# Three edits in one kernel: memory preparation inside the first gemm, the first gather beside the router, expert scatters by matmul at seven pairs

## The chip, the cores and the metric

One NeuronCore of a Trainium2 chip. The metric is the device time of one execution in microseconds (us): the median of three runs. The profile is one further execution, with its own time.

The engines are PE (matrix multiply, into PSUM), DVE (elementwise, reductions), ACT (activations, copies), POOL (elementwise, and DMAs with indices), SP (here only a queue that issues DMAs). The kernel uses eight PSUM banks: four named pmm, three paux, one pacc.

## The reference

Two blocks over x (512 tokens of 1024). What touches the change:

```
first block:  h = rms_norm(x); u, v, sq, sk, sv, mq, z = split(h @ w_in)      # widths 512,512,256,128,128,256,1024
  y_a = gelu(u) * (w_spatial(causal) @ layernorm(gelu(v)) + b)                # in chunks of 128 tokens
  y_b = sliding window attention(sq, sk, sv) + relative bias, 4 heads
  mk, mv = split(rms_norm(mem) @ w_mem_kv);  y_c = attention(mq, mk, mv)      # mem: 256 rows of 1024
  x = x + rms_norm((concat(y_a, y_b, y_c) * silu(z)) @ w_out)
second block: sparse attention and a state space branch, merged (not touched), then the experts:
  g = argmax of 4 group logits; 2 best of the group's 8 experts; weights by softmax
  out[token] = sum over its 2 experts of  (silu(h @ gate_e) * (h @ up_e) * weight) @ down_e     # 32 experts, 1024 -> 256 -> 1024
  x = x + out
```

All arithmetic is float32. The 32 experts' weights are 192 units of 128x1024 (512 KB): per expert four of gate and up, two of down.

## The kernel before, in words

Most gemms split each operand into a high and a low part of a faster float type and run three products (L224 to L226, L269 to L271, L315 to L317). The weights are loaded raw (tile tb), copied to whi (L173, ACT) and subtracted to wlo (L175, DVE or POOL). The expert products take the raw float32 weights.

**Order.** The program is traced once in the order in which it is written, and a planner then gives each engine its queue: among the instructions that its own model of time calls ready it takes the one written first. Tiles of one tag (t2, tb, xe, y) share a fixed number of buffers. `mix(main, filler)` interleaves two generators: for each microsecond that a step of main asks for, steps of filler are written behind it. Within `manual_schedule(engines)` the written order holds on those engines.

**First block (L524 to L829).** x is loaded in eight pieces and split; eight squares are summed on POOL (L393). The first gemm (`gemm_r2`, L561) makes v for the gate; its norm comes in at its last step (L558). The memory rows are loaded on POOL's queue (L571). Then the products for k and v, q of the window, q of the memory (f1, L632) are written as filler of the layer norm (`ln_chain`) and the memory preparation (`mem_prep`, L574: square, split, sum, norm). `q_done` (L606) multiplies a product by the norm, which frees its PSUM banks, and stacks it. Behind that stand the bias, the memory's two gemms (L644, L645), and the attention of eight units, mixed with the gemms of u (two) and z (two); z[2] and z[3] follow.

**Router (`block2c`, L1402; `route`, L1525).** The last gemm runs in halves of 256 tokens; each half's tokens are transposed to rows (`rows`), its logits go to the plog bank and through `route`: on DVE the group maximum, the two best, one-hot rows; a small product on PE (L1563 to L1568) counts positions, giving posm. `moe_start` (L1853) asks for the first ten weight units, `moe` for eight more.

**Experts (`moe`, L1874).** Experts go in 16 pairs; each expert has 64 slots, 32 for each half of the tokens. `prep` writes the one-hot matrix of eight experts (L1657) and the slot weights; `gather_h` (first eight experts, by halves) and `gather` (the next groups, one group ahead) bring token rows to slots by matmul (L1709, L1725). Per pair: `gate_up` (L1738, 16 products), `act_t`, then one pair later `down` (L1759, 8 products). A weight tile that is used up is asked for anew by SP (`pair`, `moe_fetch`), 18 tiles in rotation.

The results of pairs 0 to 11 are stored in slot order to scratch memory (`y_store`), and after pair 11 each token fetches its two rows by index (`y_fetch`, L1780, eight fetches of 512 KB); a token whose expert is in another pair reads row 0 and multiplies it by zero. The results of pairs 12 to 15 are split (`y_split`) and added by matmul with the transposed one-hot rows (`slots_t`, `scatter`, `finish`): 12 and 13 together, then 14 and 15, and the rows go out.

```
        f1 = chain(self.gemm_t(u1(2), hh, hl, KK, kv_done), self.gemm_t(u1(3), hh, hl, KK, q_done(sq)),
                   self.gemm_t(u1(4), hh, hl, KK, q_done(mq)))
        mix(chain(self.ln_chain(av, vc), mem_prep()), f1)
```

Of the kernel before, what the change touches and what calls it, by code (L numbers as in the profile page):

```python
# [19 lines left out]
P = 128  # L20
T = 512
# [22 lines left out]
class Ker:  # L44
# [479 lines left out]
    def block1(self):  # L524
# [36 lines left out]
        run(self.gemm_r2([u1(0), u1(1)], hh, hl, [av_done(0), av_done(1)], norm))  # L561
        rb, rbh = r["b"], r["bh"]
        self.rvt1 = self.rows("rv1", self.px, nc.sync)

# [27 lines left out]
        m = {}  # L592
        skh, skl, sq, mq, mkh, mkl = [], [], [], [], [], []
# [40 lines left out]
        mix(chain(self.ln_chain(av, vc), mem_prep()), f1)  # L634
# [8 lines left out]
        nc.any.tensor_copy(sv, self.tpose([m["svT"][:, t * P:(t + 1) * P] for t in range(NT)]))  # L643
        run(self.gemm_t([("wm", 0), ("wm", 1)], mh, ml, KK, mk_done, n=256))  # L644
# [7 lines left out]
        st = {}  # L652
# [87 lines left out]


        ya = []
        bsp = self.rv("b_s").rearrange("p (g t) -> p g t", g=4)

        def u_done(g):
            def f(ps):
                us = [self.t2() for _ in range(2)]
                for u, p in zip(us, ps):
                    nc.vector.tensor_tensor(u, p, rb, op=ALU.mult)
                ss = []  # L750
                for c in range(2):
                    gi = 2 * g + c
                    pm = self.paux()
                    for t in range(NT):
                        nc.tensor.matmul(pm[:, t * P:(t + 1) * P], vc[t][:, gi * P:(gi + 1) * P],
                                         wtri[:, gi * P:(gi + 1) * P], start=True, stop=True)
                    s = self.t2()
                    nc.vector.tensor_tensor(g4(s), g4(pm), bsp[:, gi:gi + 1].to_broadcast([P, 4, P]), op=ALU.add)
                    ss.append(s)
                self.gelu2(us)  # L760
                for u, s in zip(us, ss):
                    nc.vector.scalar_tensor_tensor(s, s, 0.5, u, op0=ALU.mult, op1=ALU.mult)
                    ya.append(s)
            return f
# [3 lines left out]
        def z_done(g):  # L768
            def f(ps):
                zs = self.silu_from(ps, rbh)  # L770
                for c, z in enumerate(zs):
# [630 lines left out]
    def block2c(self, mh, ml):  # L1402
# [67 lines left out]
        for _ in self.route(0, self.rms_sum(self.ssq3, 0)):  # L1470
            pass
        rows(3, 0, 2)
# [4 lines left out]
        with self.norm1(True):  # L1477
# [21 lines left out]
            run(r)  # L1499
            self.route_end()  # L1500
# [24 lines left out]
    def route(self, h, pc):  # L1525
# [44 lines left out]
        nc.vector.tensor_tensor(self.posm[:, ts], pp[:, :64].rearrange("p (t e) -> p t e", t=2), mb, op=ALU.mult)  # L1570
        nc.vector.tensor_reduce(self.r["mx"][:, h:h + 1], pp[:, 64:96], axis=AX.X, op=ALU.max)
# [48 lines left out]
    def route_slots(self):  # L1620
# [13 lines left out]
        nc.vector.tensor_scalar(ok, sl, 1.0, None, op0=ALU.is_ge)  # L1634
        nc.vector.scalar_tensor_tensor(ok, sl, 64.0, ok, op0=ALU.is_le, op1=ALU.mult)
        nc.vector.scalar_tensor_tensor(ok, r["ei"], 24.0, ok, op0=ALU.is_lt, op1=ALU.mult)
        nc.vector.scalar_tensor_tensor(rw, r["ei"], 64.0, sl, op0=ALU.mult, op1=ALU.add)
        nc.vector.scalar_tensor_tensor(rw, rw, -1.0, ok, op0=ALU.add, op1=ALU.mult)
# [12 lines left out]
    def prep(self, b):  # L1651

        nc = self.nc
        oh = self.pg.tile([P, NT, 256], F32R, tag="oh", name=self.nm("oh"), bufs=1)
        for t in range(NT):
            i = self.iota1[:, t // 2 * 32:t // 2 * 32 + 32]
            nc.vector.tensor_tensor(oh[:, t].rearrange("p (e s) -> p e s", s=32),  # L1657
                                    i.unsqueeze(1).to_broadcast([P, 8, 32]),
                                    self.posm[:, t, 8 * b:8 * b + 8].unsqueeze(2).to_broadcast([P, 8, 32]),
                                    op=ALU.is_equal)  # L1660
        yield oh
        pc = self.paux()
        for q in range(2):
            for t in range(NT):
                o = 12 * (t // 2 * 2 + q)
                nc.tensor.matmul(pc[:, o:o + 12], oh[:, t, q * P:(q + 1) * P], self.wc[:, t, :, 12 * b + 6 * q:12 * b + 6 * q + 6],
# [17 lines left out]
    def slots_t(self, p):  # L1684
# [7 lines left out]
        o = self.pg.tile([P, T], F32R, tag="ohT", name=self.nm("ohT"), bufs=self.no)  # L1692
# [3 lines left out]
    def xtile(self, xe):  # L1696
        xe.append(self.pg.tile([P, 8, 64], F32, tag="xe", name=self.nm("xe"), bufs=self.nxe))

    def gather_h(self, oh, xe):

        nc = self.nc
        for h in range(2):
            for d in range(8):
                if h == 0:
                    self.xtile(xe)
                pg = (self.pmm if d % 2 else self.paux)()[:, :256]
                for t in (2 * h, 2 * h + 1):
                    for j, src in enumerate((self.hth, self.htl)):
# [491 lines left out]
```

## Time and profile before

| | |
|---|---|
| median of 3 runs | 1332.47 us (1329.52 to 1336.8) |
| profiled execution | 1331.22 us, span 1329.6 us, mean granted PE clock 0.981 |
| busy, share of the span | PE 1258.4 (95%), DVE 861.8 (65%), ACT 506.9 (38%), POOL 440.0 (33%) |
| DMA moved | 224.86 MB, mean 169 GB/s; in the expert slices mostly 415 to 416 |
| issues | 82 + 55 + 55 weight units of 512 KB, 12 stores and 8 fetches of results |

The span runs from the first to the last instruction of the core; the execution's time has 1.6 us around it. A line number is a line of the kernel before, and often a helper's. In a row, `out<-in` are tile names. `[2.77 <-DVE eq]` is the idle time of the engine just before the instruction, and what ended it. [...] Matmuls overlap, and a float32 product leaves two records, so the spacing of records counts and not their length.

### The profile page before, as it was taken

What the parts mean: (1) busy time and instruction counts of PE and PEld (TensorE: products, weight loads), DVE (VectorE), ACT (ScalarE), POOL (GpSimd) and SP (SyncE); (2) the same over time, 40 slices, a digit from 0 to 9 for tenths busy, and PEclk for the clock granted to TensorE, in tenths of its full rate; (3) what the DMA queues carried; (4) which work ended last, traced back from release to release, by engine and by line L of the source; (5) the groups of instructions that cost most, each with busy time, mean ns of one, the idle gap of its engine ahead of it and who ended that gap; (6) DMA issues with size and microseconds to landing.
All of it is one profiled execution on the core that took longest, in us unless ns stands there. A gap on an engine that the chain in (4) does not pass through costs nothing. (4 is left out here: it accounts for less than half of the span.)

```text
span 1329.6 us, 18774 instructions
## 1 busy us (share of the span) xinstructions
PE 1258.4 (95%) x6992; PEld 970.4 (73%) x6992; DVE 861.8 (65%) x1648; ACT 506.9 (38%) x938; POOL 440.0 (33%) x467
## 2 busy tenths in 40 slices
PE   5969999999999999999999999999999999998997
PEld 5857888989987888888777787877889744333323
DVE  5596765667999767777988788778583522111116
ACT  4535553355644455444444443443233211111011
POOL 5473133159344413113354343445324200000011
PEclk8979999999999999999999999999999899999999
DMA  7315233143233232034424334386330699999994
GB/s 253 111 54 154 64 97 110 48 145 95 79 96 119 80 97 78 25 115 125 119 88 115 107 96 135 98 280 177 122 142 24 245 416 416 397 416 415 416 414 179
DMA packets 87342, 224.86 MB, mean 169 GB/s; under 512 B 7840, under 2 KB 31040, under 8 KB 87248
## 3 DMA queue, kind: packets, MB, share of 16 engines
q1 hardware_dynamic: 79808, 203.08, 44.2%
q10 hardware_dynamic: 4992, 11.83, 2.3%
q0 software_dynamic: 2448, 8.72, 1.8%
q8 instruction: 56, 0.92, 0.3%
q14 instruction: 38, 0.31, 0.1%
HBM read 205.97 MB, written 17.63 MB: 168 GB/s over the span
## 5 line engine op out<-in xcount | busy, mean ns | idle before, releaser
L175 POOL TENSOR_TENSOR wlo<-tb,whi 128x1024 fp32r<-128x1024 f32 x78 | 199.6, 2560 | 319.5 <-ACT whi L173 293.1
L224 PE MATMUL pmm<-tb,whi 128*128 128x512 f32 x600 | 239.1, 399 | 1.8 <-DVE t L903 1.8
L225 PE MATMUL pmm<-tb,whi 128*128 128x512 f32 x600 | 237.2, 395 | 0.0
L226 PE MATMUL pmm<-tb,wlo 128*128 128x512 f32 x600 | 236.8, 395 | 0.0
L173 ACT CAST whi<-tb 128x1024 fp32r<-128x1024 f32 x139 | 145.0, 1046 | 143.4 <-PE pmm L225 57.1
L224 PEld LDWEIGHTS pmm<-tb,whi 128*128 128x128 f32 x600 | 114.0, 190 | 25.5 <-DVE t L903 2.2
L226 PEld LDWEIGHTS pmm<-tb,wlo 128*128 128x128 f32 x600 | 113.8, 190 | 23.8 <-issue 0.2
L225 PEld LDWEIGHTS pmm<-tb,whi 128*128 128x128 f32 x600 | 113.8, 190 | 23.1 <-issue 0.7
L175 DVE TENSOR_TENSOR wlo<-tb,whi 128x1024 fp32r<-128x1024 f32 x61 | 82.2, 1349 | 27.8 <-ACT whi L173 27.4
L224 PE MATMUL pmm<-t,whi 128*128 128x512 f32 (+1 forms) x208 | 80.2, 393 | 12.4 <-DVE t L610 12.4
L225 PE MATMUL pmm<-t,whi 128*128 128x512 f32 (+1 forms) x208 | 80.3, 389 | 0.8 <-DVE t L356 0.8
L226 PE MATMUL pmm<-t,wlo 128*128 128x512 f32 (+1 forms) x208 | 80.0, 388 | 0.0
L1745 DVE SCALAR_TENSOR_TENSOR th<-th,pmm 128x256 f32<-128x256 f32 x16 | 6.7, 420 | 102.6 <-ACT th L1744 102.6
L1262 DVE TENSOR_SCALAR t<-t,acs 128x128 f32<-128x128 f32 x128 | 41.8, 393 | 26.9 <-DMA t<-scr_a 26.7
L1183 DVE SCALAR_TENSOR_TENSOR t<-cv,cwh,t 128x512 f32<-128x512 f32 x72 | 58.5, 868 | 0.3 <-ACT t L1180 0.3
L1677 POOL COPY wcol<-wrow 32x2 f32<-32x2 f32 x64 | 12.0, 188 | 135.7 <-DVE y L1771 57.0
L1738 PE MATMUL pmm<-wr,xe 128*64 128x512 f32 x200 | 55.6, 597 | 0.6 <-DMA wr<-in_we_dram 0.6
L224 PEld LDWEIGHTS pmm<-t,whi 128*128 128x128 f32 x208 | 40.1, 193 | 20.0 <-issue 12.8
L334 PE MATMUL pmm<-whi,tb 128*128 128x256 f32 x192 | 54.7, 285 | 0.0
L336 PE MATMUL pmm<-whi,tb 128*128 128x256 f32 x192 | 54.5, 284 | 0.0
L335 PE MATMUL pmm<-wlo,tb 128*128 128x256 f32 x192 | 54.3, 283 | 0.0
L1744 ACT ACTIVATE th<-pmm,wcol 128x256 f32<-128x256 f32 x16 | 7.6, 474 | 113.1 <-PE pmm L1738 56.1
(446 smaller groups left out, 2969.2 us busy)
## 6 DMA issues: line engine op xcount, KB each, us to landing
wr<-in_we_dram SPq DMA_DIRECT2D x82, 512.0 KB, 10.0
tb<-in_w_dram SPq DMA_DIRECT2D x78, 512.0 KB, 3.7
rx<-in_we_dram SPq DMA_DIRECT2D x55, 512.0 KB, 9.0
tb<-in_we_dram SPq DMA_DIRECT2D x55, 512.0 KB, 10.1
tb<-in_wo_dram SPq DMA_DIRECT2D x16, 512.0 KB, 3.7
tb<-in_wg_dram SPq DMA_DIRECT2D x16, 512.0 KB, 3.6
t<-scr_a SPq DMA_DIRECT2D x16, 512.0 KB, 6.4
tb<-in_wsb_dram SPq DMA_DIRECT2D x16, 512.0 KB, 4.1
```

The lines of the kernel that those rows point to most:

```text
L173: nc.vector.tensor_copy(hi, raw) if dve_hi else nc.scalar.copy(hi, raw)
L175: f = lambda: (nc.gpsimd if pool_lo else nc.vector).tensor_tensor(lo, raw, hi, op=ALU.subtract)
L224: nc.tensor.matmul(ps[c][:, :n], hi[:, s], xh[k], start=first, stop=False)
L225: nc.tensor.matmul(ps[c][:, :n], hi[:, s], xl[k], start=False, stop=False)
L226: nc.tensor.matmul(ps[c][:, :n], lo[:, s], xh[k], start=False, stop=last)
L334: nc.tensor.matmul(o, xh[k][:, ts], hi[:, s], start=(k == 0 and t % 2 == 0), stop=False, **kw)
L335: nc.tensor.matmul(o, xh[k][:, ts], lo[:, s], start=False, stop=False, **kw)
L336: nc.tensor.matmul(o, xl[k][:, ts], hi[:, s], start=False, stop=(k == 7), **kw)
L1183: nc.vector.scalar_tensor_tensor(y, x[:, i:T + i], w(ct, i), y, op0=ALU.mult, op1=ALU.add)
L1262: nc.vector.tensor_scalar(h8(ab)[:, h], h8(ab)[:, h], self.acs[:, c, 8 * g + h:8 * g + h + 1], 0.0, op0=ALU.subtract, op1=ALU.min)
L1677: nc.gpsimd.tensor_copy(w[o:o + 32, i // 2, 0:2], wrow[e * 32:e * 32 + 32, 2 * h + q, e:5:4 - e])
L1738: nc.tensor.matmul(pg[h * 64:h * 64 + 64], xe[d][:, e + h], w[:, j * 512:(j + 1) * 512], start=(d == 0), stop=(d == 7))
```

## The change

**First block.** The loads of mem are written ahead of the first gemm, and the preparation is mixed into that gemm from its third step on; f1 is filler of the layer norm alone. The first u gemm, with its part of the gate, is written ahead of the memory's gemms. The attention's filler is the second u gemm and z[0], z[1], z[2].

**Router.** The one-hot of the first half (`oh_half(0, 0)`) is written ahead of the rows of the last 256 columns. Of `route(1)` only the part to the norm stays in `block2c`; then `moe` writes the first half's gather, the rest of the route, the second half's one-hot and gather, with all engines in written order.

**Experts.** PE is in written order to the end of the stage. Nine more weight units are loaded ahead, once, into three y, four xe and two ohT buffers, beside the 18 in rotation. Seven pairs (3, 6, 9, 12 to 15) are scattered by matmul, each for itself and two pairs after its products; nine are stored. Fetches have a bounds check: a token without a stored row has an index above the bound and its row is not moved; their four tiles are zeroed first. The one-hot is two tiles (one per half), xe eight double tiles, ohT two double tiles. `finish` begins the first four groups of pair 14 ahead of the last down products, and folds the residual by matmul in two groups instead of one.

```diff
@@ block1
-        run(self.gemm_r2([u1(0), u1(1)], hh, hl, [av_done(0), av_done(1)], norm))
...
+        f0 = self.gemm_r2([u1(0), u1(1)], hh, hl, [av_done(0), av_done(1)], norm)
+        for _ in range(2):
+            next(f0)
+        mix(mem_prep(), f0)
+        run(f0)
...
-        mix(chain(self.ln_chain(av, vc), mem_prep()), f1)
+        mix(self.ln_chain(av, vc), f1)
...
+        run(self.gemm_t(u1(5), hh, hl, KK, u_done(0)))
         run(self.gemm_t([("wm", 0), ("wm", 1)], mh, ml, KK, mk_done, n=256))
...
-        f2 = chain(*[self.gemm_t(u1(5 + g), hh, hl, KK, u_done(g)) for g in range(2)], z[0], z[1])
+        f2 = chain(self.gemm_t(u1(6), hh, hl, KK, u_done(1)), z[0], z[1], z[2])
         mix(self.pipeline(units, (logits, expo, ptrans, pvmul, otrans), 4.5), f2)
         run(f2)
-        run(z[2])
@@ block2c
         for _ in self.route(0, self.rms_sum(self.ssq3, 0)):
             pass
+        self.oh0 = self.oh_half(0, 0)
...
-            run(r)
-            self.route_end()
+            self.rt = r
@@ route_slots
+        nc.gpsimd.memset(base, 16384.0)
...
+        nc.vector.tensor_scalar(t2, ok, -16384.0, 16384.0, op0=ALU.mult, op1=ALU.add)
+        nc.vector.tensor_tensor(rw, rw, t2, op=ALU.add)
@@ oh_half, new
+        o = (self.pg if h else self.pa).tile([P, 2, 256], F32R, tag=f"slot{h}", name=self.nm("oh"), bufs=1)
+        for t in range(2):
+            nc.vector.tensor_tensor(o[:, t].rearrange("p (e s) -> p e s", s=32), i,
                                    self.posm[:, 2 * h + t, 8 * b:8 * b + 8].unsqueeze(2).to_broadcast([P, 8, 32]),
                                    op=ALU.is_equal)
@@ y_fetch
-            y = self.ytile()
+            y = self.yf[t % 2 * 2 + j]
-                ap=self.row1[:, t, j:j + 1], axis=0))
+                ap=self.row1[:, t, j:j + 1], axis=0), bounds_check=18 * 64 - 1, oob_is_err=False)
@@ finish
+        for t in range(NT):
+            early(0, t)
+        yield 1
+        for t in (0, 1):
+            early(1, t)
+        for t in range(NT):
+            late(0, t)
+        for t in (0, 1):
+            late(1, t)
+        for t in (2, 3):
+            early(1, t)
+            late(1, t)
@@ moe_start, moe_fetch
+        self.extra = [("y", self.ny)] * 3 + [("xe", self.nxe)] * 4 + [("ohT", self.no)] * 2
...
+            if n <= u < n + m:
+                tag, bufs = self.extra[u - n]
+                t = self.pg.tile([P, 1024], F32, tag=tag, name=self.nm("wr"), bufs=bufs)
+                self.nc.sync.dma_start(t, self.a["we"][e, i])
@@ moe, moe_body
+        self.direct = [3, 6, 9, 12, 13, 14, 15]
+        for _ in range(2 * self.nw + len(self.extra)):
+            self.moe_fetch()
+        with self.tc.manual_schedule(engines={pe}):
+            with self.tc.manual_schedule(engines=set(other)):
+                xe = []
+                self.gather_h(self.oh0, xe, 0)
+                next(self.rt)
+                next(self.rt)
+                oh = self.oh0, self.oh_half(0, 1)
+                run(self.rt)
+                self.route_end()
+                self.gather_h(oh[1], xe, 1)
+            self.moe_body(oh, xe)
...
+            if p == 16:
+                fin = self.finish()
+                next(fin)
+            if p:
+                if p == 1:
+                    ac = next(at.pop(0))
+                py = [self.pmm() for _ in range(2)]
+                for k in range(2):
+                    self.down(py, pair(p - 1, 4 + k), ac, k)
+                (self.y_split if p - 1 in self.direct else self.y_store)(p - 1, py)
+                if p < 16:
+                    ac = next(at.pop(p))
...
+                    if i == 2:
+                        xn = []
+                        gg = self.gather(oh, 8, xn)
+                    some(gg, 4)
+            if p > 1 and p - 2 in self.direct:
+                run(self.scatter((p - 2,)))
+            if p < 15 and p + 1 in self.direct:
+                self.slots_t(p + 1)
+            if p == 12:
+                self.yf = [self.pg.tile([P, 1024], F32, tag="xe", name=self.nm("yf"), bufs=self.nxe) for _ in range(4)]
+                for y in self.yf:
+                    nc.gpsimd.memset(y, 0.0)
@@ setup
-    k.fold = [(0, 0)]
+    k.fold = [(0, 3), (1, 1)]
-    k.nrx, k.ny, k.nxe, k.no = 5, 5, 16, 4
+    k.nrx, k.ny, k.nxe, k.no = 5, 5, 8, 2
```

## Rows read from the trace of the kernel before

**Rows 1.** The page's 40 slices: busy tenths of the 16 DMA engines.
```profile
DMA  7315233143233232034424334386330699999994
```

**Rows 2.** PE's waits, 0 to 200 us: us in total, times, longest.
```profile
PE pmm L224 <- DVE t L610: 12.4, 1, 12.4
...
PE pmm L316 <- DVE wlo L175: 6.1, 2, 5.7
```

**Rows 3.** Timeline of DVE, 60 to 135 us: start, us, line, [idle before <-releaser].
```profile
79.05 0.88 DVE L359 SCALAR_TENSOR_TENSOR t<-t,pvt,t 128x256 fp32r<-128x256 f32 x2
...
90.48 1.28 DVE L610 TENSOR_TENSOR t<-pmm,tb 128x512 f32<-128x512 f32 x2
```

**Rows 4.** Front: busy (x) of PE, PEld, DVE, ACT, POOL; PEclk, DMA, GB/s.
```profile
91.00:96.00 5.00, 4.70 (x24) 4.73 (x25) 4.23 (x8) 3.51 (x5) 1.06 (x1) 0.56 0.24 89
...
16.00:20.00 4.00, 1.61 (x10) 1.00 (x8) 4.00 (x4) 3.66 (x5) 3.84 (x4) 1.00 1.03 409
...
20.00:24.00 4.00, 0.00 (x0) 0.00 (x0) 4.00 (x2) 1.04 (x1) 4.00 (x3) 0.54 0.36 146
...
32.00:36.00 4.00, 4.00 (x35) 4.00 (x35) 0.00 (x0) 0.56 (x1) 0.00 (x0) 1.00 0.00 0
```

**Rows 5.** The same view and columns, from the router on.
```profile
1044.00:1048.00 4.00, 4.00 (x21) 4.00 (x21) 3.17 (x26) 0.95 (x3) 0.00 (x0) 0.53 0.56 226
...
1056.00:1064.00 8.00, 8.00 (x40) 2.69 (x38) 1.25 (x4) 0.47 (x1) 2.09 (x12) 1.00 0.83 273
...
1051.00:1288.00 237.00, 225.47 (x999) 92.63 (x999) 46.04 (x108) 31.65 (x62) 17.49 (x71) 0.99 1.00 399
```

**Rows 6.** Timeline of PE at the router.
```profile
1043.15 0.77 PE L1709 MATMUL paux<-oh,tb 128*128 128x256 f32 x2 [2.77 <-DVE eq L1546]
```

**Rows 7.** Chain of waits in order of time: start, us, what.
```profile
1054.26 13.88 PE pmm L1738 x64
...
1072.25 3.58 PE pmm L1759 x16
...
1082.70 0.37 PE paux L1750 x2
...
1084.01 1.88 PE paux L1725 x16
...
1176.01 11.36 DMA tb<-in_we_dram
...
1269.49 15.25 DMA wr<-in_we_dram
...
1286.36 0.47 PE paux L1837 x2
...
1313.87 1.86 PE pmm L1759 x4
...
1322.67 1.21 PE pacc L1808 x4
```

**Rows 8.** Timeline of SP's queue: start, us, line, x issues.
```profile
1033.72 4.81 SPq L1850 DMA_DIRECT2D wr<-in_we_dram  x4
...
1056.15 3.76 SPq L1850 DMA_DIRECT2D tb<-in_we_dram  x5
...
1292.44 1.61 SPq L1850 DMA_DIRECT2D wr<-in_we_dram  x2
```

**Rows 9.** The page's DMA issues: KB each, median us to landing.
```profile
wr<-in_we_dram SPq DMA_DIRECT2D x82, 512.0 KB, 10.0
...
scr_y<-y ACTq DMA_DIRECT2D x12, 512.0 KB, 7.0
```

**Rows 10.** Timeline of POOL, 0 to 60 us.
```profile
19.35 2.79 POOL L175 TENSOR_TENSOR wlo<-tb,whi 128x1024 fp32r<-128x1024 f32 x1
...
43.68 2.39 POOL L571 DMA_DIRECT2D t<-in_memT_dram  x4
```

**Rows 11.** Timeline of PE in the expert stage.
```profile
1246.16 3.40 PE L1759 MATMUL pmm<-rx,ac 128*64 128x512 f32 x4
```

More of the change, by code (lines that the diff above doesn't have):

```diff
@@ L651, in block1 @@
         sinks = self.rv("sinks")
-        st = {}
+        st, done = {}, set()
         def logits(u):
@@ L739, in otrans @@
                                   po[:, :256].rearrange("p (c t) -> p c t", c=2))
[L742 to L764, printed above, removed]
+            done.add(u)
         yh, yl = [], []
@@ L1691, in slots_t @@
         nc.tensor.matmul(pt, sel, self.posT, start=True, stop=True)
-        o = self.pg.tile([P, T], F32R, tag="ohT", name=self.nm("ohT"), bufs=self.no)
+        if self.direct.index(p) % 2 == 0:
+            self.oht = self.pg.tile([P, 2 * T], F32R, tag="ohT", name=self.nm("ohT"), bufs=self.no)
+        c = self.direct.index(p) % 2 * T
+        o = self.oht[:, c:c + T]
         nc.vector.tensor_scalar(o, pt, self.iotac, None, op0=ALU.is_equal)
@@ L1771, in y_store @@
         nc.vector.tensor_scalar(y[:, 512:], py[1], w, None, op0=ALU.mult)
-        nc.scalar.dma_start(self.y1d[p * P:(p + 1) * P], y)
+        n = sum(q not in self.direct for q in range(p)) * P
+        nc.scalar.dma_start(self.y1d[n:n + P], y)
     def y_fetch(self, t):
@@ L1787, in y_split @@
         w = self.wcol[p][2]
-        if p < 14:
-            q4 = [self.pg.tile([P, 512], F32R, tag="xe", name=self.nm("yq"), bufs=self.nxe) for _ in range(4)]
-            hs, ls = q4[:2], q4[2:]
-        else:
-            h, l = self.ytile(F32R), self.ytile(F32R)
-            hs, ls = ([x[:, :512], x[:, 512:]] for x in (h, l))
+        h, l = self.ytile(F32R), self.ytile(F32R)
+        hs, ls = ([x[:, :512], x[:, 512:]] for x in (h, l))
         for q in range(2):
@@ L1909, in moe @@
                     self.gate_up(pg, pair(p, j), xe, 2 * i, j)
+                if p == 0:
+                    run(pre)
                 at[p] = self.act_t(pg, *self.wcol[p][:2])
@@ L1915, in moe @@
+            if p == 16:
+                run(fin)
+                break
+            if g < 3:
+                if i == 0:
                     pre = self.prep(g + 1)
                     oh = next(pre)
-                elif i == 1 and g < 3:
+                elif i == 1:
                     run(pre)
-                    xn = []
-                    work.append(self.gather(oh, 8, xn))
-                if p == 14:
-                    for k in range(12, 16):
-                        self.slots_t(k)
@@ L1924, in moe @@
-                if p == 15:
-                    work.append(self.scatter((12, 13)))
-            if p:
-                ac[p - 1] = next(at.pop(p - 1))
-                some(3 if p < 16 else 100)
-                if p == 16:
-                    work.append(self.finish())
-                py = [self.pmm() for _ in range(2)]
-                for k in range(2):
-                    self.down(py, pair(p - 1, 4 + k), ac[p - 1], k)
-                    if p == 16:
-                        some(2)
-                if p < 13:
-                    self.y_store(p - 1, py)
-                else:
-                    self.y_split(p - 1, py)
-                if p in (13, 14):
-                    for t in range(2):
-                        self.y_fetch(2 * (p - 13) + t)
@@ L1945, in moe_more @@
+            if p in (13, 14):
+                for t in range(2):
+                    self.y_fetch(2 * (p - 13) + t)
     def moe_more(self):
```

185 lines of the change are left out of this document (105 added, 80 removed).

## The prediction

> **What bounds the kernel now.** I read the 40 slices first: DMA is low up to slice 31 and at its top only from slice 33 on, while the page has PE busy nearly throughout [rows 1]. So there are two regimes, and the change touches both, in three places.
>
> Front. Among PE's waits up to 200 us look at the largest, 12.4 us of L224 (the gemm for the memory keys) for DVE's L610 [rows 2]. DVE's timeline says why: it is never idle there, and from 79.05, where the layer norm is done, to 90.48, where the first L610 stands, it does the memory preparation (L359, L393) [rows 3]. What PE waits for is PSUM: of the four pmm banks two hold the q product until q_done (L610) has read it. After that stretch without work the granted clock is 0.56 from 91 to 96 us [rows 4].
>
> Router. PE runs out of work at 1040.4 and waits 2.77 us for the router's DVE chain; the first gather half then runs at a clock of 0.53, and the first expert product starts at 1054.26 [rows 5 to 7]. DMA runs dry in the same stretch: 18 weight tiles were asked for by 1038.5, all have landed by about 1046, and the next issue is at 1056.15, when a tile is free again [rows 5, 8].
>
> Experts. In the chain of waits PE's work ends at 1176; from there to 1284 it is weight copies alone [rows 7]. The last weight is asked for at 1293.7; with the median landing time of 10.0 that is 1303.7. PE is behind by then: down products until 1315.7, then the last scatters until 1323.9; the span ends 5.7 us later, at 1329.6 [rows 7 to 9].
>
> **The change part by part.** Front, (a) the stall. The memory preparation is emitted inside the first gemm instead of behind the layer norm, so the DVE work of rows 3 goes from there. In the new place there is room: from 32 to 36 us DVE does nothing and ACT 0.56 [rows 4]; that idle stretch of DVE lasts from 28.2 to 42.4. The work is 8 x 0.44 (L359), 3 x 0.61 (L393) and some 0.7: 6 us, hidden. It needs its data early, though. The four loads went out on POOL at 43.68, right behind the power of the first norm, although they read nothing of it [rows 10]: t2 buffers are handed out in the order of first writes, and av's first write (43.74) stood before them. Now it stands behind, so the loads can go at about 17 us, once the eight squares are out. L610 then follows the layer norm at 79.0 and takes 1.28, and PE goes on at 80.3: 12.4 shrinks to 1.4. The slow stretch goes too: 4.7 busy at 0.56 would be 2.6 at full clock, -2.1. What is late next is vc, whose last POOL step ends at 88.5, before u_done wants it at 91. (b) The price is four issues on POOL, 2.39 together, ahead of its weight splits (19.35 and the next), while PE waits 5.7 us for a split in L316 [rows 2, 10]: between 0 and 2.4; I take 1.2, since the split that PE waits for last is DVE's. (c) u1(5) ahead of the memory gemms and z[2] among the attention's fillers move PE work within a stretch that has no gaps: 0, hidden by gemms of some 11 us each; if that cover is gone, 3 either way. Front: -11.0 - 2.1 + 1.2 = -11.9, taken as -12, bounds -15 and 0.
>
> DMA share is 1.03 at 409 GB/s from 16 to 20 us, but 0.36 from 20 to 24 [rows 4]. [...]
>
> Router. The gather of the first half now stands on PE right behind the router's small matmuls. At full clock 16 of its matmuls take 1.88 [rows 7], 32 take 3.8, from 1039.9, beside the DVE chain, where PE idled. The chain is rid of two L1657 (0.41 each) that were threaded into it, and its position product runs at about 1044.9 instead of 1048.1, behind the slow gather. Then posm 0.2, the second oh_half 0.8 and the second half 3.8: the first expert product starts at 1050, or 1053 if the clock falls in the gap from 1043.8 to 1046, against 1054.26. In a stage that DMA sets this is worth only weight tiles freed earlier: -1, bounds -4 and 0.
>
> Experts, the weight stream. (d) Nine more tiles can be asked for before the first is freed (buffers of y, xe and ohT not yet in use). They lie over buffers of the stages before, whose last readers end by 1042.1, before DMA runs dry. At the 416 GB/s of the page's slices a 512 KB tile takes 1.26 us, nine 11.3: as long as the gap from 1046 to 1057. The ramp behind the gap, 273 instead of 416 GB/s for 8 us [rows 5], cost 2.7 and goes too. (e) Seven pairs instead of four are scattered by matmul, so nine stores instead of twelve [rows 9]: -3.8. (f) Fetches: five of eight lay ahead of the last weights, 6.3; now all eight do, with the rows of direct pairs left out, 9/16 x 8 x 1.26 = 5.7: -0.6, or +3.8 if a row left out takes its time all the same. Last weight: 1303.7 - 11.3 - 2.7 - 3.8 - 0.6 = 1285.3.
>
> (g) PE in that time [rows 7]: per pair 6.94 (half of 13.88) + 3.58 + 0.37, times 16 is 174; three gathers of 7.5, 23; preps and slots 6; seven scatters of 16 x 0.235 = 3.8, 26 (15 before); folds 2: 231, of which 222 are ahead of the last down product. From 1051 that ends at 1273, 12 before the last weight: DMA still sets the end, though not by much. PE's order is now written by hand, so a matmul whose operand is late holds all that is queued behind it (weight products, transposes, scatters), and the DVE adds of 0.68 and SP's next issues wait for those. I put 1.5 on it, bounds 0 and 10.
>
> (h) The tail. Ahead of down(15) PE has transposes 0.4, scatter(13) 3.8 and pair 14's first matmuls 2.8, and can start them 3.2 before the last weight; it comes to down(15) at +3.7, ends it at +7.3, waits 1.9 for the split (1315.7 to 1317.5 before), and ten groups of 0.47 and the 5.7 of before make +19.6. Before it was 1329.6 - 1303.7 = 25.9. So -6.3: the scatter of 12 and 13 and the fetch adds are out of it.
>
> Sum of the experts: 1285.3 + 19.6 + 1.5 = 1306.4 against 1329.6, -23.2; router -1; front -12; together -36: a span of 1293.4, with the 1.6 that the profiled run has around its span 1295. That run (1331.2) lies 1.3 below the median of 1332.5, so I say 1297.
>
> **The rivals.**
> A, the front stall finds another cause. DVE has no idle time from 49 to 79 either; if mem lands late, or its splits are ordered behind the norm's products, the same DVE work stands ahead of L610. For: the loads were held by an order, not by data. Against: 14 us of idle DVE. Front 0: 1309.
>
> B, the stream gets no lead. If the nine buffers come free only with the router's last readers (1049 to 1053), SP, which issues in order, stands still as it did and the 11.3 + 2.7 stay: 1311. Against: what lies under them belongs mostly to the gemm that ended at 1037.
>
> C, slower: the hand order on PE and the clock. Where PE waits for a weight nothing else fills in, and its clock goes down. For: at 1246.16 four records took 3.40 us where 16 take 3.58 [rows 7, 11]. Against: the mean clock of the stage is 0.99 [rows 5]. Each us of expert matmuls at half clock costs one more; 12 are free and 36 gained, so it decides from 48 us on, a fifth of the 222. At a quarter (55 us): 1297 + 55 - 12 = 1340.
>
> [...]
>
> D, it doesn't do what it says: a row left out takes its time in the queue, 4.4 with (f): 1301.
>
> **How the numbers follow.** Forecast 0.61 (its own range 1288 to 1305, from the bounds of b, g and the router), A 0.13, B 0.13, C 0.05, D 0.08. The range reaches to A and B, 1286 to 1313; left out are C, A and B together (1323), and the last fifth of a better front. A difference of 0.5%, 6.7 us, is what a measurement can tell from none. Faster: forecast, D, A and B but for the 0.03 where these meet, 0.92. Same 0.03; slower 0.05 (C).
>
> **What would show it.** The gemm behind q waits under 3 us, with mem's loads out before 20: (a). First expert product 4 to 1 us earlier beside the router's end: the router. DMA at its top from the first weight tile to the last, with no hole: (d). Nine stores and 2.4 MB fetched: (e, f). PE sets the chain up to about pair 12, later than now: (g). A clock under 0.9 in the expert slices proves C. The forecast is wrong if the end moves by less than 20 us.

## The result, and the profile after

The changed kernel takes 1315.11 us (median of 4 runs, 1313.75 to 1318.53), the kernel before 1332.79 beside it: a ratio of 0.987, 95% interval 0.9836 to 0.9904. The end moved by 17.7 us, where 36 were forecast. One execution of e5 and one of e6 below were disturbed (over 2000 us) and are left out of the ratios and of the medians given (with them 1297.07 and 1316.78); e6's profile was that one and is not read.

The profiled execution has a span of 1312.0 us. The page's slices of the clock (PEclk: the granted clock as a share of full speed, here in tenths) and of DMA, which answer to [rows 1]:

```profile
PEclk8999999989999999999999999999999999999889
DMA  7224242142224222033434335385430999999992
```

DMA is now at its top from slice 32 on, right behind the empty slice 31, where before it took a slice to get there: the lead of (d). In the last slice it does half as much (2 for 4): the end belongs to TensorE. PE's waits up to 200 us, which answer to [rows 2] (us in total, times, longest):

```profile
PE pmm L316 <- DVE wlo L175: 10.1, 2, 9.6
PE pmm L315 <- ACT whi L173: 9.2, 3, 8.0
PE paux L481 <- issue: 2.7, 1, 2.7
```

The 12.4 us behind L610 are gone. Two others have come or grown: L316 waits 9.6 instead of 5.7, and L481 (the bias rows) waits 2.7. The stretch that follows the second, to be read with [rows 4]:

```profile
94.00:110.00 16.00, 16.00 (x65) 11.47 (x65) 9.28 (x11) 2.22 (x3) 12.54 (x9) 0.71 0.34 115
```

PE is busy throughout but at a granted 0.71: 0.50 from 94 to 103.4, 1.00 from 104 to 110. The last of the x1 stores, the end of the front, is issued at 274.4 instead of 277.8. Then PE's waits from 1020 us to the end (the largest two):

```profile
PE paux L1869 <- ACT xe L1752: 8.3, 1, 8.3
PE pacc L1869 <- DVE acc L1871: 4.2, 1, 4.2
```

The first of them stands in PE's timeline in the middle of pair 9's scatter (start, us, what, [idle before <-releaser]):

```profile
1212.47 0.63 PE L1869 MATMUL paux<-y,ohT 128*128 128x512 f32 x2
1221.38 1.22 PE L1869 MATMUL paux<-y,ohT 128*128 128x512 f32 x2 [8.28 <-ACT xe L1752]
```

and ACT's timeline says what was late:

```profile
1208.89 0.37 ACT L1777 COPY ac<-paux 128x256 f32<-128x256 f32 x1 [0.59 <-PE paux L1775]
1220.37 0.33 ACTq L1798 DMA_DIRECT2D scr_y<-y  x1
1220.74 1.07 ACT L1752 COPY xe<-paux 128x512 f32<-128x512 f32 x2 [11.47 <-DMA wr<-in_we_dram]
```

ACT finished its copies at 1209.3 and then stood for 11 us before it could issue a store whose data was long there; the gather's copies (L1752), queued behind the store, hold the banks that the scatter wants. What releases ACT is the landing of a weight tile. In the trace the weight loads and the stores raise the same eight DMA semaphores (counters that rise as a transfer lands), the loads in turn, and each of the nine stores waits for the one that it raises itself. Here the load that last took it was issued at 1210.19 and raised it 16 times from 1218.23 to 1220.27, and the store went out at 1220.37; eight of the nine went out 0.10 us after such a rise.

This wait is not new. In the kernel before, six of the twelve stores stood 6.8 to 9.2 us on ACT in the same way, the one at 1210.12 for 7.5:

```profile
1210.12 0.33 ACTq L1772 DMA_DIRECT2D scr_y<-y  x1
1210.49 0.47 ACT L1744 ACTIVATE th<-pmm,wcol 128x256 f32<-128x256 f32 x1 [7.89 <-DMA tb<-in_we_dram]
```

PE lost less by it there, 2.50 us at most in that stage; behind the store above:

```profile
1212.00 0.44 PE L1750 MATMUL paux<-cst,th 128*128 128x128 f32 x2 [2.34 <-DVE th L1746]
```

What is new is that copies which PE's hand-written order cannot pass stand behind the store (in e7 below, with the planner's order, no such wait of PE is over 1.5 us). The second wait is on DVE:

```profile
1264.10 1.29 DVE L1871 TENSOR_TENSOR acc<-paux,acc 128x512 f32<-128x512 f32 x2 [0.28 <-PE paux L1869]
1265.31 2.60 DVE L1808 SCALAR_TENSOR_TENSOR acc<-yf,has,acc 128x1024 f32<-128x1024 f32 x2
1267.94 0.69 DVE L1871 TENSOR_TENSOR acc<-pacc,acc 128x512 f32<-128x512 f32 x1
1268.55 2.59 DVE L1808 SCALAR_TENSOR_TENSOR acc<-yf,has,acc 128x1024 f32<-128x1024 f32 x2
```

Four adds of fetched rows (L1808) stand between the scatter's adds. SP's queue, which answers to [rows 8], asks for the last weights 22 us earlier than before:

```profile
1029.99 10.88 SPq L1909 DMA_DIRECT2D wr<-in_we_dram  x9
...
1268.30 2.90 SPq L1882 DMA_DIRECT2D tb<-in_we_dram  x3
```

With the page's 10.1 us to landing the last is there at 1281, and the kernel ends 31 us later, where the forecast's (h) gave 19.6. The expert stage, to be read with the last of [rows 5]: a lower clock. (The changed kernel is 9 us further on in this window, and its stream ends at 1281 within it; from 1042 to 1281 its DMA share is 1.01 at 401 GB/s, no lower than before.)

```profile
1051.00:1288.00 237.00, 221.55 (x1052) 98.42 (x1052) 83.14 (x160) 34.07 (x65) 26.72 (x81) 0.96 0.98 391
```

### The profile page after: what moved, and what is told of

Its sections match the earlier page's. It is cut to its first block, busy times and chain, and to the rows that moved or that the text cites. A ratio compares the mean times of both kernels' runs of the same rounds, so it can differ in the third digit from the quotient of the medians.

```text
span 1312.0 us, 18947 instructions
## 1 busy us (share of the span) xinstructions
PE 1246.0 (95%) x7045; PEld 974.2 (74%) x7045; DVE 883.3 (67%) x1690; ACT 509.1 (39%) x942; POOL 446.7 (34%) x484
## 3 DMA queue, kind: packets, MB, share of 16 engines
q0 software_dynamic: 2448, 6.77, 1.4%
## 5 line engine op out<-in xcount | busy, mean ns | idle before, releaser
L1763 PE MATMUL pmm<-wr,xe 128*64 128x512 f32 x240 | 66.4, 595 | 0.0
L1055 ACT ACTIVATE tL<-tL,xm 128x128 f32<-128x128 f32 (+3 forms) x64 | 35.4, 554 | 31.7 <-DVE xm L1047 31.5
## 6 DMA issues: line engine op xcount, KB each, us to landing
wr<-in_we_dram SPq DMA_DIRECT2D x89, 512.0 KB, 10.1
tb<-in_we_dram SPq DMA_DIRECT2D x53, 512.0 KB, 10.1
```

The costliest lines, as they stand in the source:

```text
L1763: nc.tensor.matmul(pg[h * 64:h * 64 + 64], xe[d][:, e + h], w[:, j * 512:(j + 1) * 512], start=(d == 0), stop=(d == 7))
```

## The experiments

Each median stands beside runs of the kernel before on the same chip (1329.8 to 1332.8); the intervals are about 4 us wide to either side, so that 3 us between two medians say little, and single stages are read from the traces. How far one trace can be trusted is seen where the code is the same: the front ends between 267.6 and 274.4 in eight traces (changed kernel, e3, e4, e7, e10, e12, e13, e14), the experts take 337.5 to 340.7 in five (changed kernel, e1, e2, e8, e11), and the stretch between the two, which no edit touches, takes 694.7 to 705.4. "Front" is the last x1 store, "experts" the time from the first x1 load (L1423) to the end: 274.4 and 339.2 in the changed kernel, 277.8 and 347.8 before.

**e8**, the front as before, in the changed kernel: `block1` replaced by the old one.

> The changed kernel with block1 as it was before (mem's chain beside gemm f1, mem's loads behind it, the order of u's gemms as before); router and experts are the changed ones. It prices the front's part of the change as a whole. Theory: the front's stall of 12.4 us and its slow stretch are removed, but 4.2 us of a later start and 8 us around the wait for onehot are paid for it, so the front is worth 3 us: 1318.5 (1316 to 1321). Prediction's step (a) to (c): it is worth 13 to 14: 1328 (1326 to 1330). Rival: its gain is lost in the later stages' order: 1315 within 1.5.

1320.54 us, front 279.7. The front's part of the change is worth 5.4 by the medians and 5.3 by the traces, not 12.

**e1**, the onehot table early.

```
-        oh = self.t2()[:nb, :384]            # in rel_bias
-        nc.scalar.dma_start(oh, a["onehot"])
+        self.oh1 = self.t2()[:a["rel_bias"].shape[0], :384]   # in block1, ahead of f1
+        nc.sync.dma_start(self.oh1, a["onehot"])
```

> The changed kernel, with the onehot table that rel_bias reads loaded early through SP's queue, ahead of the gemms of k, v and q; in the changed kernel its load stands on ACT's queue behind a chain of casts and is issued at 90.57 us. Theory: in the changed kernel the 12.4 us stall on L610 is gone, and a new one took its place: TensorE waits 2.74 us on L481 at 93.73 for this table, and then runs at the granted 0.71 from 94 to 110 (L291 to L293 take 330 ns instead of 283 to 296, L481 842 ns instead of 481). Then the wait is gone, PEclk is above 0.95 in 94 to 110, the x1 stores come about 8 us earlier (5 to 9), and the end moves from 1315 to 1307 (1305 to 1311). Rival: something else is late in the same place (the bias rows' own chain, a bank), the front gains under 2 us and the end stays within 2 us of 1315.

1311.96 us (ratio 0.9837). L481's wait is gone; its place was taken by the next table on ACT's queue (wspT), whose product PE waits 3.0 us for, and PEclk is 0.89 from 94 to 110. Front 271.6, 2.8 earlier, which is within what the unchanged front does: between theory and rival, since both were true in turn.

**e2**, mem's loads from SP.

```
-            nc.gpsimd.dma_start(t, a["memT"]...)    # ahead of mem_prep
+                nc.sync.dma_start(t, a["memT"]...)  # in mem_prep's first step
```

> The changed kernel, with mem's four loads issued from SP's queue (behind seven weight tiles, ahead of the eighth) instead of POOL's, where they are issued at 14.6 to 17.0 us. The first gemm resumes at 29.19 us in the changed kernel, 24.95 before. Theory: POOL's four issues push its adds and its subtracts together, from 17.0 to 27.4 us, and DVE, beside them, needs 8.8 us for one L359 (0.74 to 2.8 us otherwise), so that the six L359 take 15.55 us instead of 10.58. Then these six take 10 to 11.5 us again, TensorE resumes at 25 to 26.5, the x1 stores come 3 to 4 us earlier, and the end goes from 1315 to 1311.5 (1310 to 1313). Rival: the loads' 1 MB of the DMA engines' time ahead of the last of the first gemm's weights is what is late (its cast starts at 24.11 instead of 21.35): TensorE resumes at 27.5 to 29 and the end moves by under 2 us.

1311.19 us (ratio 0.9838), front 266.9. The six L359 in DVE's timeline, first e2, then the changed kernel:

```profile
12.41 10.59 DVE L359 SCALAR_TENSOR_TENSOR tb<-t,pvt,tb 128x512 fp32r<-128x512 f32 x6 [0.62 <-ACT tb L358]
```

```profile
12.45 15.55 DVE L359 SCALAR_TENSOR_TENSOR tb<-t,pvt,tb 128x512 fp32r<-128x512 f32 x6 [0.62 <-ACT tb L358]
```

PE resumes at 25.26 instead of 29.19, as the theory had it. That alone does not put the rival out: in e2 the loads went out behind the weight that the first gemm waits for last, whose cast starts at 21.75 again instead of 24.11. Two later runs, whose front is that of the changed kernel, tell the two apart. In e13 and e14 (below) the four issues stand on POOL and the cast is as late (24.48 and 24.43), but the six L359 take 10.27 and 10.25 us; e13:

```profile
12.41 10.27 DVE L359 SCALAR_TENSOR_TENSOR tb<-t,pvt,tb 128x512 fp32r<-128x512 f32 x6
```

PE resumes at 26.0 and 26.2 there, and the front ends at 267.6 and 268.2. So DVE's loss is what holds PE, and not the late weight; and the four issues don't force it. With them on POOL it came in seven of nine traces (15.2 to 15.6 us), without them in none of six.

**e3**, the y stores from POOL.

```
-        nc.scalar.dma_start(self.y1d[n:n + P], y)
+        nc.gpsimd.dma_start(self.y1d[n:n + P], y)
```

> The changed kernel, with the nine y stores (L1798) issued from POOL's queue instead of ACT's. Theory: ACT issues its instructions in order, and a store's issue there waits for the landing of a weight tile that was asked for shortly before it (idle 8.3, 9.1, 11.5, 12.7 and 11.5 us before the issues at 1124.5, 1140.9, 1172.5, 1188.8 and 1220.4); the gather's copies (L1752) stand behind the store, and TensorE, in its order written by hand, waits 8.28 us for them at 1221.4. Then ACT has no idle time of over 4 us that ends with a DMA, TensorE's wait on L1869 for ACT's xe is under 1 us, PEclk is 1.00 from 1200 to 1230, and the end moves from 1315 to 1306 (1303 to 1309). Rival 1: the weights set the end anyway, so that the 8 us come back as a wait on DMA further on: end within 2 us of 1315. Rival 2: POOL's issues (1.0 to 1.2 us each) hold DVE, and the stall only moves: 1313 to 1318.

1308.17 us (ratio 0.9823). The 8.28 us wait is gone, PE is busy 35.3 of 36 us from 1200 to 1236 at a clock of 1.00. Then PE meets the stream (waits for weights of up to 1.0 us, 4.3 in all) and the L1808 adds (6.1). Experts 336.3: 2.9 of the 8.3 are kept, little more than the spread.

**e4**, the adds of the fetched rows behind pair 12's scatter, DVE's order by hand from pair 14 on.

```
+            if p == 14:
+                hand.enter_context(self.tc.manual_schedule(engines={nc.vector.engine}))
...
-            if p in (13, 14):
-                for t in range(2):
-                    self.y_fetch(2 * (p - 13) + t)
+            if p == 13: fetch 0, 1
+            if p == 14: add 0, fetch 2, add 1, fetch 3, add 2, add 3
```

> The changed kernel, with the eight adds of the fetched rows (L1808, 1.28 us each) moved behind pair 12's eight scatter adds on DVE, in an order written by hand from pair 14 on. Theory: four of these adds stand between the scatter adds in the changed kernel, so that TensorE waits 4.16 and 0.78 us for a bank at 1268.7 and 1272.4, falls to the granted 0.59 from 1266 to 1274, and starts the last pair's gate_up at 1274.27 though its weights are there. Then these waits are under 1 us in all, the last gate_up starts 5 us earlier, and the end moves from 1315 to 1309 (1307 to 1312). Rival: the last weight tile, asked for at 1271.2, or the late fetches (the last lands at about 1282) set the end, and at most 2 us are gained.

1310.13 us (ratio 0.9842), but experts 338.4, 0.8 less, which is no difference: what the median gained is not in this stage. PE's largest waits there show why:

```profile
PE paux L1775 <- DVE th L1771: 8.6, 1, 8.6
PE paux L1873 <- ACT xe L1752: 8.3, 1, 8.3
```

The scatter's wait is gone and a new one stands at the last pair: its activation waits on DVE behind adds whose rows land late. That was the rival.

**e6**, no early tiles.

```
-        self.extra = [("y", self.ny)] * 3 + [("xe", self.nxe)] * 4 + [("ohT", self.no)] * 2
+        self.extra = []
```

> The changed kernel without the nine weight tiles that it asks for ahead of the experts in buffers of y, xe and ohT (18 tiles instead of 27). The prediction's step (d) priced them at 11.3 us plus 2.7 of the ramp. Theory: in the changed kernel TensorE, not the stream, sets the end (the last pair begins 3 us after its weights are there, and TensorE waits under 2 us in all for weights), so the nine tiles' lead is worth less than that: the stream without them ends about 11 us later, at about 1292, and TensorE's end follows by the part that its stalls don't cover, 3 to 8 us: 1318 to 1323. The prediction's own view: the stream sets the end, and the full 11 to 14 us come back: 1326 to 1329. Rival: the buffers free up late anyway and the lead is lost by 1100: 1315 within 2.

1316.6 us (ratio 0.9892): the nine tiles are worth 1.5 in the changed kernel, within the error of nothing; less than the theory's 3 to 8, though the interval reaches into it.

**e7**, TensorE's order left to the planner in the expert stage: `self.moe_body(oh, xe)` moved out of `manual_schedule(engines={pe})`.

> The changed kernel, with the order of TensorE's work in the expert stage left to the planner instead of the order written by hand (the router's part stays as it is). Theory: the hand-written order only costs where something late stands in it (8.28 us at 1221 and 5.2 us at 1269 to 1273); the planner, which places work by modelled due times, has waits of its own (before: six of up to 2.3 us on th), so the end stays within 6 us of 1315, 1312 to 1321, with the long wait on the gather's copies under 4 us. Rival: the hand order itself is what lost the time, and the planner's is faster by the two stalls: 1302 to 1308.

1331.35 us, ratio 0.9998 (0.9976 to 1.002): as slow as the kernel before, outside both. The late waits are gone (PE waits 7 us in all in this stage), but down's products are busy 101.1 us (the sum of its three groups) where the changed kernel has 71.0; first e7, then the changed kernel:

```profile
L1784 PE MATMUL pmm<-wr,ac 128*64 128x512 f32 x116 | 42.6, 600 | 0.5 <-ACT ac L1777 0.5
L1784 PE MATMUL pmm<-tb,ac 128*64 128x512 f32 x92 | 38.0, 600 | 0.0
L1784 PE MATMUL pmm<-rx,ac 128*64 128x512 f32 x48 | 20.5, 597 | 0.0
```

```profile
L1784 PE MATMUL pmm<-wr,ac 128*64 128x512 f32 x116 | 31.2, 594 | 0.7 <-ACT ac L1777 0.5 <-DMA wr<-in_we_dram 0.2
L1784 PE MATMUL pmm<-tb,ac 128*64 128x512 f32 x92 | 24.6, 598 | 0.7 <-DMA tb<-in_we_dram 0.7
L1784 PE MATMUL pmm<-rx,ac 128*64 128x512 f32 x48 | 15.2, 597 | 0.1
```

The timeline of e7 shows 8 records (four of each expert of the pair) in 1.94 us, and 4 alone in just as much, when scatters (L1869) or transposes (L1775) stand between:

```profile
1115.34 1.94 PE L1784 MATMUL pmm<-tb,ac 128*64 128x512 f32 x8
1117.21 0.73 PE L1869 MATMUL pacc<-y,ohT 128*128 128x512 f32 x2
1117.87 1.93 PE L1784 MATMUL pmm<-tb,ac 128*64 128x512 f32 x4
1119.73 0.44 PE L1775 MATMUL paux<-cst,th 128*128 128x128 f32 x2
1119.93 1.17 PE L1869 MATMUL paux<-y,ohT 128*128 128x512 f32 x4
1121.02 1.93 PE L1784 MATMUL pmm<-tb,ac 128*64 128x512 f32 x4
```

**e10**, the loops of down swapped.

```
-        for q in range(2):
-            for h, w in enumerate(ws):
+        for h, w in enumerate(ws):
+            for q in range(2):
```

> The changed kernel with the two loops of down (L1784) swapped: both products of one expert's weights first, then both of the other's; same matmuls, same place in the hand order. With TensorE's order left to the planner (e7) the kernel takes 1331, as long as before, and TensorE hardly waits in it (7 us in all): its L1784 is busy 101.1 us in place of 71.0. Theory: the two experts of a pair write different halves of the 128 columns; records of different halves that follow each other run side by side (16 in 3.60 us), records of the same half one after the other (4 in 1.93), and it is this neighbourhood that the hand order keeps and the planner's breaks. Then here L1784 is busy 100 to 125 us, and the end comes 25 to 50 us later: 1340 to 1365. Rival: the planner's order is slower for other reasons (gathers and scatters between the products, late transposes): L1784 stays within 5 us of 71 and the end within 4 us of 1315.

1312.13 us (ratio 0.984), L1784 busy 72.6, 16 records in 3.65: refuted. The order of the halves inside one group does not matter.

**e13 and e14**, small full-width products between the halves, or behind both. They compute nothing that is used.

```
         for h, w in enumerate(ws):
             for q in range(2):
                 nc.tensor.matmul(py[q]...)
+            if spare:                                     # e13
+                nc.tensor.matmul(self.paux()[:, :12], self.ident, self.ident[:, :12], ...)
+        for _ in range(2 * spare):                        # e14 instead
+            nc.tensor.matmul(self.paux()[:, :12], self.ident, self.ident[:, :12], ...)
```

> The changed kernel with the loops of down swapped as in e10, and one small product of full width (128 columns, 12 wide, read by nobody) behind each half's two products, 60 in all (pairs 0 to 14). e10 showed that the order inside the 16 records of a pair's down doesn't matter (3.65 us against 3.60). Theory, as it is left: two halves' records run side by side as long as nothing of full width stands between them; in the planner's order (e7, and the kernel before) scatters, gathers and transposes stand there, and each half then takes 1.93 us alone (4 records). Then here L1784 takes 4 x 1.93 = 7.7 us a pair, its busy time is 71 + 15 x 4.1 = 130 us (110 to 135), and the end comes 45 to 75 us later than that of its control e14: 1365 to 1395. Rival: the small products cost only themselves: L1784 stays within 5 us of 71, the end within 5 us of the control.

> The control to e13: the same 60 small products, but two behind both halves of each step of down, so that the halves stay neighbours. Both theories: 60 x 0.13 to 0.26 = 8 to 16 us more of TensorE, and two steps a pair instead of one group of 16: L1784 busy 71 to 76 us, the end at 1315 to 1331.

e13 takes 1369.46 us (ratio 1.0272, 1.0248 to 1.0296), e14 1315.39 (0.9871, 0.9841 to 0.99): 54 us for the place of the same 60 products. L1784 is busy 120.7 and 71.5 us. First e13, then e14:

```profile
1127.17 1.88 PE L1784 MATMUL pmm<-tb,ac 128*64 128x512 f32 x4
1128.98 0.39 PE L1787 MATMUL paux<-cst 128*128 128x12 f32 x2
1129.31 1.93 PE L1784 MATMUL pmm<-tb,ac 128*64 128x512 f32 x4
```

```profile
1126.91 1.94 PE L1784 MATMUL pmm<-wr,ac 128*64 128x512 f32 x8
1128.78 0.61 PE L1787 MATMUL paux<-cst 128*128 128x12 f32 x4
```

So it is shown here: the two experts' products run side by side, 8 records in 1.94 us, while nothing of full width (128*128) stands between them; with the small product between, 4 records take 1.88 to 1.93. The kernel before has such lone groups too; one stands two rows behind that of [rows 11]:

```profile
1249.90 1.93 PE L1759 MATMUL pmm<-rx,ac 128*64 128x512 f32 x4
```

**e11, e12 and e5**: the front's waits taken away, the experts', and both. e11 is e1 and e2 with wspT loaded early too; e12 is e3 with the adds moved thus:

```
+            if p == 13:
+                hand.enter_context(self.tc.manual_schedule(engines={nc.vector.engine}))
...
+            if p == 13: fetch 0, 1; add 0, fetch 2, add 1, fetch 3
+            if p == 14: add 2, add 3
```

> The changed kernel with e5's three early loads of the front alone (onehot and wspT through SP ahead of the gemms of k, v and q; mem's loads through SP); experts as in the changed kernel. Theory: the front and the experts add up; the front's part of e5 is the 8 us by which its x1 stores come earlier (266.4 against 274.4): 1307 (1304 to 1310). Rival: e2 and e1 alone had already brought 3 to 4 each in the median, one of them by chance of the run, and the front gives 4: 1311.

> The changed kernel with e5's two edits of the experts alone (y stores from POOL; the adds of the fetched rows where DVE is idle); front as in the changed kernel. Theory: the waits behind the store and behind the adds stand in series, so that taking away one of them (e3, e4) only lets TensorE meet the next, and both together give more than their sum: x1 loads to the end 329 instead of 339, the end at 1305 (1302 to 1308). Rival: the gains of e3 (7 in the median) and e4 (5) add up: 1303 or less; or the stream sets the end at once: 1310 or more.

> The changed kernel with all the waits taken away that its trace shows as new: the onehot and wspT tables loaded early through SP, mem's loads from SP, the y stores from POOL, and the adds of the fetched rows ahead of pair 14's activations on DVE, in an order written by hand from pair 13 on, where DVE has nothing to do (4 of them beside pair 14's gate_up, 4 beside pair 15's). Theory: the prediction's account of what the change removes was right, and what it missed are these waits: front about 6 earlier (e1 gained 3 at the x1 stores and lost 3 again to the wait for wspT's product), start 0 to 4, stores 4, adds 4 to 6; the end at 1297 (1291 to 1302), the prediction's 1297 with it. Rival: the stream of weights, which runs without a hole, sets the end as soon as the waits are gone, and the gains of the expert stage (8 to 10) shrink to those of the stores alone: 1302 to 1306.

e11 1308.93 (ratio 0.9814, front 265.9), e12 1303.99 (0.9794; x1 loads to the end 330.4), e5 1296.27 (0.9728, 0.9689 to 0.9766; front 266.4, experts 329.2). They add up: 6.2 and 11.1 of the changed kernel's time alone, 18.8 together. Within the experts the two edits of e12 give 8.8, where e3 and e4 alone gave 2.9 and 0.8: the two waits stand in series, as the theory had it. e5 beats both kernels, and lies where the prediction was. PE's largest waits in e5 from 1020 us on are for weights again:

```profile
PE pmm L1764 <- DMA wr<-in_we_dram: 2.0, 2, 1.2
PE pmm L1764 <- DMA tb<-in_we_dram: 1.3, 2, 1.0
PE pmm L1785 <- DMA tb<-in_we_dram: 1.1, 2, 0.8
```

**e9**, e5 without the nine tiles (`self.extra = []`).

> e5_all without the nine weight tiles asked for early. Without them the changed kernel itself lost only 1.7 us (e6), where the prediction's step (d) gave them 11.3 and 2.7. Theory: they are worth that only when the stream of weights sets the end, and in the changed kernel TensorE's waits did; with the waits gone the end follows the stream and comes 8 to 14 us later: 1308 (1304 to 1311). Rival: the lead is lost on the way whatever TensorE does, since a tile can be asked for again only when TensorE has read it: within 3 us of e5, 1295 to 1300.

1303.74 us (ratio 0.9793), experts 334.7 against 329.2. With the waits gone the tiles are worth 7.5 in the medians, 5.5 in the stage: rather less than the theory's 8 to 14, and not nothing. SP's queue says the same: counted from the first x1 load, the last weight is asked for at 302.4 in e9 and at 297.2 in e5, so that 5.2 of the 11.3 us of lead reach the end. That the tiles are worth more in e5 than in the changed kernel is not shown, since the intervals of the two differences overlap.

## Why the prediction was wrong

What it says the change removes, it removes; what it missed are the waits that the change brings or lets PE meet. Of the 18.3 us between forecast and result e5 gives back 18.8 in the medians, by taking away those waits and nothing else.

By stages the sums look thus. The forecast was 12 for the front and 24.2 from the x1 loads on (router and experts). The trace of the changed kernel has 3.4 and 8.6, and 5.6 more in the untouched stretch between; that of e5 has 11.4 and 18.6, and 3.4 between. So a part of each total is luck, and that e5 ends where the forecast was does not prove its terms. Of the 24.2, the last weight was to be asked for 19.4 earlier, counted from the x1 loads, and it came 13.8 earlier (e5 14.7); what stands behind it was to be 4.8 shorter, and it grew by 5.2 (e5: 3.9 shorter).

**Front.** (a) The stall went, by the mechanism named: mem's preparation runs at 30 to 36 us, hidden. The slow stretch came back in another place, behind L481: the onehot table stands on ACT's queue behind the casts of q; its load goes out at 90.57 instead of 101.7, but PE wants it 14 us earlier than before. This is rival A's way, a new cause after the old one; (a) named vc as the next thing that is late and forgot the tables. What the wait costs differs from execution to execution (see the last section). (b) failed in its mechanism: I bounded POOL's four issues by their own time (0 to 2.4) and asked only what POOL's splits lose. What lost was DVE: beside POOL's work, which runs back to back as it did before, one L359 takes 8.81 us, from 17.52 on, where in the kernel before none of the six took over 2.83. POOL and DVE of the changed kernel:

```profile
17.02 1.70 POOL L393 TENSOR_TENSOR t<-t,t 128x512 f32<-128x512 f32 x1
18.69 2.34 POOL L175 TENSOR_TENSOR wlo<-tb,whi 128x1024 fp32r<-128x1024 f32 x1
21.00 1.25 POOL L393 TENSOR_TENSOR t<-t,t 128x512 f32<-128x512 f32 x1
22.22 2.33 POOL L175 TENSOR_TENSOR wlo<-tb,whi 128x1024 fp32r<-128x1024 f32 x1
24.52 2.93 POOL L393 TENSOR_TENSOR t<-t,t 128x512 f32<-128x512 f32 x2
```

```profile
17.52 8.81 DVE L359 SCALAR_TENSOR_TENSOR tb<-t,pvt,tb 128x512 fp32r<-128x512 f32 x1
```

PE resumed 4.2 us later than before; with the issues gone (e2) it did not, but in e13 and e14, with the same four issues, it resumed only 1.1 and 1.2 later, and the six L359 took 10.27 and 10.25 us. POOL's rows above stand one right behind the other all through the 8.81 us; why DVE took that long beside them, and what decides between the two, stays open. (c) was not tried alone. Front: 12 forecast, 5.4 measured (e8), 11.6 with the waits gone (5.4 and e11's 6.2); e13 and e14 show that most of these 6.2 can also come with no edit of the front.

**Router.** Right: first expert product at 1043.7, of which 9.0 was there already at the x1 loads; 1.6 belong to this step.

**Experts.** (d) The lead came: 27 tiles asked for by 1040.9 and DMA without a hole. Its price was mis-sized. The 11.3 and 2.7 us were to reach the end whole: 1.5 measured in the changed kernel, 5.5 (stage) to 7.5 (medians) without the waits. (e) Nine stores, as forecast, but their price was put at transfers alone. A store also needs its turn on ACT, where it stood 8 to 13 us in five of nine cases (6.8 to 9.2 in six of twelve before, where it could have been read); this step and (g) failed together. (f) 6.77 MB went through the software queue, which took 8.72 before. A row left out leaves a packet of 4 bytes with a median of 9 ns in place of one of 4 KB with 162, so rival D is out.

(g) is the step that failed most. Stalls in the hand-written order were put at 1.5, bounds 0 to 10; they are 8.3 and 5.2, with PE at a granted 0.59 to 0.76 around them, and e12 prices them at 11.1 in the medians, 8.8 in the stage. I had named what would be queued behind a late operand, but looked for late weights and not for a late copy. The sum of 231 us for PE was about right for a reason that I did not see. I took 3.58 us for 16 records of down from a row of [rows 7] where they stood undisturbed; on average the kernel before took more (L1759 is busy 99.4 us in its trace), and it is the hand-written order that makes all of them so cheap. Without it (e7) the whole change is worth nothing. The row of [rows 11], 4 records in 3.40 us, I read as the clock, for rival C; 4 records alone take 1.93 at full clock, so the clock (0.61 from 1246 to 1250) made them 1.8 times as long, and standing alone 2.2 times. It fell behind a wait of 1.57 us for DVE's th, not for a weight, and ahead of that th stood a store on ACT, issued at 1243.09: the row that I took for rival C was the wait that (g) forgot.

(h) 31 us behind the last weight instead of 19.6, because DVE's fetch adds stood in pair 12's scatter and the last pair began late; in e5 it is 22 (last weight asked for at 1264.2, landing 10.1 later, end 1296.2).

**Rivals.** B did not happen as told: the tiles came free in time. C's mechanism, an operand that holds all of PE's order, is what happened, at 9 to 11 us instead of 55, and the same order is worth 16. By its own last sentence, an end that moves by under 20 us, the forecast was wrong.

## What to carry to other kernels

When an edit takes a wait away, list for each engine behind it what is issued in order there, loads of small tables and stores included: the next thing that is late is there, and it can cost its own wait and a slow clock behind it (here 2.6 to 3.0 us, and a granted 0.70 to 0.89 over the next 16). A lead in a stream is worth what the other engines don't lose again; price it by what is left of it at the last load (5.2 of 11.3 us here), and read in the old trace which waits stand there already and cost little as yet. Products of 64 columns (128*64) belong, by e13 and e14, next to those of the other expert, with nothing of full width (128*128) in between: 1.94 us for 8 records, where 4 alone take 1.93.

## What was not expected of the hardware

- Two groups of 4 records, one of each expert (128*64), take 1.94 us together, and one alone 1.93: with a full-width product of 0.39 us between them they take twice as long (e13 against e14, 54 us).
- In nine profiles PE has the same wait of 2.6 to 3.0 us on L481. Over the 16 us behind it the granted clock was 0.70 to 0.71 in three (changed kernel, e3, e10), 0.79 in one (e12) and 0.89 in five (e2, e4, e7, e13, e14). What decides it stays open. DVE's long L359 comes and goes with the same code too. Where the front's code is the same, it ended between 267.6 and 274.4; this is a good part of the spread between runs, and of e4's gain.
- ACT sat idle for up to 12.7 us ([12.73 <-DMA rx], around the store at 1188.79) until a weight tile landed that the store has nothing to do with.
